# Sums of squares by TensorE, and the order of the first pair of weight blocks, in a two-block transformer kernel

## The chip, the cores and the metric

One core of one Trainium2 chip runs the whole program. The metric is the device time of one execution in microseconds (us): 2955.29 is the median of three runs before the change (2952.16 to 2956.52). The engines are TensorE (PE, with its weight loads as PEld), VectorE (DVE), ScalarE (ACT), GpSimd (POOL) and SyncE (SP), which issues most transfers.

## The reference, cut to what matters

Two transformer blocks of two layers each work on 256 tokens `x` and 256 context tokens `ctx` of width 1024, in float32. The part that the change touches is the very first step, the first half of the first feed-forward layer:

```python
def rms_norm(x, g):
    y = x * rsqrt(mean(x * x, axis=-1) + EPS)
    return y * g
def modulate(h, shift, scale):
    return h * (1 + scale) + shift
mod = silu(c) @ w_ada[l] + b_ada[l]              # nine chunks of 1024: shift, scale, gate, ...
a, b = split(modulate(rms_norm(h, g), mod[0], mod[1]) @ w_in, 2)   # w_in is 1024 x 5632
h = h + 0.5 * mod[2] * ((silu(a) * b) @ w_out)
```

Tokens and context have modulations of their own (`c` and `c_ctx`), and the same weights.

## The kernel before

Activations lie transposed: eight tiles `h` of 128 features by 512 columns, the first 256 columns being the tokens (stream 0) and the last 256 the context (stream 1). Products are made in three passes of a reduced-precision type: weight and operand are each split into a high and a low part, `wh`, `wl` and `xnh`, `xnl`, and PE adds high x high (line 346), high weight x low operand (347) and low weight x high operand (348). ACT writes the high parts (316 for weights, 613 for operands), DVE the low parts (317, 614).

The start of the program is written apart, by the class `Start` and `first_pair` (line 758). `load_stream` (1724) has PE transpose the tokens tile by tile (1735), DVE copy each tile into `h` (1736) and `Sumsq.add` form the squares: ACT squares (98, 101), DVE adds the squares up (103) and squares the last tile (106), into buffers of which there are two. `rstd_bc` then sums over features on PE with a column of ones (568), DVE takes the inverse root with three rounds of Newton's method on two columns (580 to 588), and PE spreads it to rows (562).

The modulation's first two chunks are made in four parts, each for two tiles of `h`: PE multiplies 2 MB of `w_ada` by the padded silu (173, tile `ada`), DVE copies the result (176, `adae`), PE turns it (178, `adat`), and DVE adds the bias (184), makes the gain (186) and for two tiles and two streams scales (139, `nt`); then ACT and DVE split the scaled tiles. I call 178 the turn of a part. The products of the first pair of weight blocks with these two tiles follow: two blocks, two halves of 128 output columns each, in the accumulators `fa`.

A scheduler sets each engine's order of the whole program from a timing model of its own; `issue_after` adds the demand that what is issued inside it stands behind a given instruction of the same engine. Before the change the first weights' split stands behind the end of the roots (`chain_end`), and the parts 1 to 3 behind the spread rows (`rows_done`); how products and modulation interleave is the scheduler's choice. Behind the pair come the second pair's products, `evac` (739) and the background task `ada_tasks`, which makes the other seven chunks on DVE (481, 483). Accumulators of PE come from one pool of five buffers.

Of the kernel before, what the change touches and what calls it, by code (L numbers as in the profile page):

```python
# [9 lines left out]
F32 = mybir.dt.float32  # L10
F32R = mybir.dt.float32r
I32 = mybir.dt.int32
AF = mybir.ActivationFunctionType
ALU = mybir.AluOpType
AX = mybir.AxisListType

P = 128
D = 1024
KT = 8
T = 512  # L20
EPS = 1e-6
D_FF = 2816
# [120 lines left out]
class Start(Norm):  # L143


    def prepare(self):
# [5 lines left out]
        nc.vector.tensor_copy(self.pad[:, :, 0:2], b.silu)  # L152
        self.gs = b.spool.tile([P, KT, 2], F32, tag="gs", name=b.name("gs"), bufs=2)

    def rstd(self, s):
        self.rb[s] = self.b.rstd_bc(self.accs[s], D)

    def load(self, g):
        w = self.b.a["w_ada"][0]
# [5 lines left out]
    def part(self, g, raws):  # L165

        b, nc = self.b, self.b.nc
        ps = b.psum("ada", "ada")
        for j, raw in enumerate(raws):
            for k in range(KT):  # L170
                for i in range(2):
                    q = 32 * (2 * j + i)
                    nc.tensor.matmul(ps[q : q + 32, :P], self.pad[:, k, :], raw[:, k, P * i : P * i + P],
                                     start=(k == 0), stop=(k == KT - 1), tile_position=(0, q))
        ev = b.ntmp("adae")
        nc.vector.tensor_copy(ev[:, :P], ps[:, :P])
        pt = b.psum("adat")
        nc.tensor.transpose(pt[:, :P], ev[:, :P], b.ident)
        mod = b.mod[self.key]
        for j in range(2):  # L180
            o = KT * j + 2 * g
            src = pt[:, 64 * j : 64 * j + 64].rearrange("p (i r) -> p i r", i=2)[:, :, 0:2]
            bias = b.vec("b_ada0", o, 2).unsqueeze(2).broadcast_to([P, 2, 2])
            nc.vector.tensor_tensor(mod[:, o : o + 2, :], src, bias, op=ALU.add)
        gain = b.vec(*self.gain, KT)[:, 2 * g : 2 * g + 2]
        nc.vector.scalar_tensor_tensor(self.gs[:, 2 * g : 2 * g + 2], mod[:, KT + 2 * g : KT + 2 * g + 2, :], 1.0,
                                       gain.unsqueeze(2).broadcast_to([P, 2, 2]), op0=ALU.add, op1=ALU.mult)
        for k in (2 * g, 2 * g + 1):
            for s in self.streams:
                self.tile(s, k, self.rb[s])  # L190
        if 2 * g + 2 == KT:
            b.mod_done.update(((self.key, self.sh_chunk), (self.key, self.sc_chunk)))
# [43 lines left out]
class Builder:  # L236
# [70 lines left out]
        self.nc.sync.dma_start(v, src.rearrange("(k p) n -> p k n", p=P))  # L307
        return raw

    def split_weight(self, raw, kts, n):  # L310
        w = kts * n
        h = self.wspl.tile([P, 2048], F32R, tag="wh", name=self.name("wh"))
        l = self.wspl.tile([P, 2048], F32R, tag="wl", name=self.name("wl"))

        for i0, i1 in self.pieces(w, 1024):
            self.nc.scalar.activation(h[:, i0:i1], raw[:, i0:i1], AF.Copy)  # L316
            self.nc.vector.tensor_tensor(l[:, i0:i1], raw[:, i0:i1], h[:, i0:i1].bitcast(F32), op=ALU.subtract)  # L317
        r = lambda t: t[:, :w].rearrange("p (k n) -> p k n", n=n)
        return Weight(r(h), r(l))

# [283 lines left out]
    def split_from(self, t, dst, k, c0, c1, bias=None):  # L604

        nc = self.nc
        h = dst.H(k, c0, c1)
        l = dst.L(k, c0, c1)
        if bias is None:
            nc.scalar.activation(h, t, AF.Copy)  # L610
            nc.vector.tensor_tensor(l, t, h.bitcast(F32), op=ALU.subtract)
        else:
            nc.scalar.activation(h, t, AF.Identity, bias=bias)  # L613
            nc.vector.scalar_tensor_tensor(l, t, bias, h.bitcast(F32), op0=ALU.add, op1=ALU.subtract)  # L614

    def norm_of(self, key, gname, gi, sh_chunk, sc_chunk, streams):

# [92 lines left out]
    def ffn(self, l, which, streams, x, nxt, side=None, start=None):  # L710
        nc = self.nc
# [5 lines left out]
        w_in = a[f"w_ffn{which}_in"][l]  # L717
# [15 lines left out]
        def weights(t):  # L733
            return [self.weight(w_in[:, o + t * P : o + t * P + 256], KT, 256) for o in (0, D_FF)]
# [23 lines left out]
        def first_pair():  # L758

            raws = [start.load(0)]  # L760
            with self.tc.issue_after(self.chain_end.ins):
                ws = weights(0)
            raws += [start.load(i) for i in range(1, 4)]
            pp = [[self.psum("fa") for _ in ws] for _ in range(2)]
            for i in range(4):
                with self.tc.issue_after(self.rows_done.ins) if i else nullcontext():
                    start.part(i, raws[i])
                for j in range(2):
                    for w, ps in zip(ws, pp[j]):
                        self.mm_feat(ps, w, j * P, x, 0, T, (2 * i, 2 * i + 1), i == 0, i == 3)  # L770
            for j in range(2):
                evac(j, *pp[j], 0, T)

# [4 lines left out]
        for t in (0, 2, 4, 6, 8):  # L778
            if start is not None and t == 0:
                first_pair()  # L780
            else:
                pair(t, t == 0)
                if start is not None and t == 2:
                    self.load_vectors(2, len(self.groups), nc.sync)
# [1087 lines left out]
```

## Time and profile before

| what | value |
|---|---|
| median of 3 runs | 2955.29 us |
| the profiled execution's own time | 2955.05 us |
| its span | 2953.3 us |
| PE busy | 2885.5 us, 98% |
| DVE busy | 2122.6 us, 72% |
| ACT busy | 1086.5 us, 37% |
| mean granted clock of PE | 0.988 |

The page of the profile is one execution; its own time lies 1.75 us above its span. Times of rows count from the span's start. In a timeline each row is a run of like instructions: start, duration, engine, line, operation, output and inputs, and in brackets the idle time of the engine just before it and what ended that. The chain of waits takes 91% of the span on PE. Granted clock 1.00 is 2.4 GHz, 0.50 is 1.2 GHz.

### The profile page before, as it was taken

The numbers are of one execution on the slowest core, as the hardware profiler recorded it, in microseconds if no ns is written. First come the engines' busy times: TensorE is split into PE (matmuls) and PEld (weight loads), VectorE is DVE, ScalarE is ACT, GpSimd is POOL, SyncE is SP. The second block draws the span as 40 slices with busy tenths as digits, with TensorE's granted clock in tenths as the row PEclk, the third lists the DMA queues.
The fourth block names the chain that finished last, engine by engine and source line by source line (L and its number), as shares of the span: only waits on it lengthen the run. The fifth ranks groups of instructions, "written<-read, shape, count | busy, mean of one in ns | idle before, by whom it ended". The sixth has DMA issues, their size and how long they took to land.

```text
span 2953.3 us, 44554 instructions
## 1 busy us (share of the span) xinstructions
PE 2885.5 (98%) x17874; PEld 2480.1 (84%) x17874; DVE 2122.6 (72%) x4323; ACT 1086.5 (37%) x1986; POOL 47.8 (2%) x83
## 2 busy tenths in 40 slices
PE   8999999999999999999989999999999999999998
PEld 6788899688888888888969999886888889996998
DVE  7878768869887698777885675437697785537665
ACT  3223235543222232222653443335342223435443
POOL 0000000000000000000000000011000000011000
PEclk9999999999999999999999999999999999999999
DMA  7655523214654446454323554202255651312553
GB/s 251 206 179 197 174 73 112 62 58 159 219 182 168 135 155 210 166 191 150 104 96 115 180 167 133 76 1 68 86 172 171 199 174 56 117 53 73 171 187 111
DMA packets 357611, 410.27 MB, mean 139 GB/s; under 512 B 24066, under 2 KB 297884, under 8 KB 357404
## 3 DMA queue, kind: packets, MB, share of 16 engines
q1 hardware_dynamic: 353512, 403.63, 41.7%
q10 hardware_dynamic: 3892, 3.78, 0.4%
q8 instruction: 141, 2.31, 0.3%
q14 instruction: 66, 0.54, 0.1%
HBM read 406.34 MB, written 1.05 MB: 138 GB/s over the span
## 4 chain that ended last, share of the span: by engine, by line
PE 91%; DVE 5%; ACT 2%; DMA 1%; issue 1%; SPq 0%; POOL 0%; ACTq 0%; DVEq 0%; POOLq 0%
PE pj L346 14%; PE pj L347 13%; PE pj L348 13%; PE fa L346 9%; PE fa L347 9%; PE fa L348 9%; PE pf L346 2%; PE pf L348 2%; PE pf L347 2%; PE sc L826 2%; PE po L858 1%; DVE wl L317 1%; PE pj L360 1%; PE pj L361 1%; PE pj L362 1%; PE pt L847 1%
## 5 line engine op out<-in xcount | busy, mean ns | idle before, releaser
L316 ACT ACTIVATE wh<-wr 128x1024 fp32r<-128x1024 f32 (+3 forms) x542 | 525.8, 1017 | 860.5 <-PE pj L347 480.1
L317 DVE TENSOR_TENSOR wl<-wr,wh 128x1024 fp32r<-128x1024 f32 (+3 forms) x542 | 624.6, 1175 | 175.0 <-ACT wh L316 172.6
L483 DVE SCALAR_TENSOR_TENSOR ad<-wr,silu,ad 128x512 f32<-128x512 f32 x784 | 547.8, 744 | 16.2 <-DMA wr<-in_w_ada_dram 16.1
L347 PE MATMUL fa<-xnl,wh 128*128 128x512 f32 (+1 forms) x1472 | 522.0, 357 | 1.9 <-DVE xnl L614 1.9
L348 PE MATMUL fa<-xnh,wl 128*128 128x512 f32 (+1 forms) x1472 | 522.1, 357 | 1.1 <-DVE wl L317 1.1
L346 PE MATMUL fa<-xnh,wh 128*128 128x512 f32 (+1 forms) x1472 | 518.7, 359 | 3.8 <-ACT xnh L613 3.0
L346 PE MATMUL pj<-gh,wh 128*128 128x256 f32 (+1 forms) x1372 | 458.0, 335 | 0.0
L347 PE MATMUL pj<-gl,wh 128*128 128x256 f32 (+1 forms) x1372 | 456.6, 333 | 0.0
L348 PE MATMUL pj<-gh,wl 128*128 128x256 f32 (+1 forms) x1372 | 456.4, 333 | 0.0
L346 PEld LDWEIGHTS fa<-xnh,wh 128*128 128x128 f32 x1472 | 274.1, 188 | 49.7 <-ACT xnh L613 4.5
L348 PEld LDWEIGHTS fa<-xnh,wl 128*128 128x128 f32 x1472 | 276.7, 188 | 44.8 <-DVE wl L317 1.5
L347 PEld LDWEIGHTS fa<-xnl,wh 128*128 128x128 f32 x1472 | 276.6, 188 | 44.3 <-DVE xnl L614 2.9
L346 PEld LDWEIGHTS pj<-gh,wh 128*128 128x128 f32 x1372 | 259.5, 189 | 28.5 <-ACT wh L316 1.6
L348 PEld LDWEIGHTS pj<-gh,wl 128*128 128x128 f32 x1372 | 259.3, 189 | 27.2
L347 PEld LDWEIGHTS pj<-gl,wh 128*128 128x128 f32 x1372 | 259.6, 189 | 26.0 <-issue 0.2
L347 PE MATMUL pj<-xnl,wh 128*128 128x256 f32 (+1 forms) x824 | 259.1, 319 | 1.9 <-DVE xnl L614 1.9
L346 PE MATMUL pj<-xnh,wh 128*128 128x256 f32 (+1 forms) x824 | 256.7, 320 | 2.7 <-ACT xnh L613 2.6
L348 PE MATMUL pj<-xnh,wl 128*128 128x256 f32 (+1 forms) x824 | 259.1, 319 | 0.0
L347 PEld LDWEIGHTS pj<-xnl,wh 128*128 128x128 f32 x824 | 155.1, 189 | 13.6 <-DVE xnl L614 2.5
L346 PEld LDWEIGHTS pj<-xnh,wh 128*128 128x128 f32 x824 | 153.4, 190 | 14.8 <-ACT xnh L613 3.3
L348 PEld LDWEIGHTS pj<-xnh,wl 128*128 128x128 f32 x824 | 155.4, 189 | 12.0
L706 DVE SCALAR_TENSOR_TENSOR h<-pj,mod,h 128x256 f32<-128x256 f32 x144 | 66.5, 480 | 112.2 <-PE pj L348 112.1
(374 smaller groups left out, 4252.6 us busy)
## 6 DMA issues: line engine op xcount, KB each, us to landing
wr<-in_w_ada_dram SPq DMA_DIRECT2D x112, 1024.0 KB, 5.1
wr<-in_w_ffn_in_dram SPq DMA_DIRECT2D x88, 1024.0 KB, 5.2
wr<-in_w_mlp_dram SPq DMA_DIRECT2D x64, 1024.0 KB, 5.5
wr<-in_w_ffn_out_dram SPq DMA_DIRECT2D x32, 1024.0 KB, 5.0
wr<-in_w_in_dram SPq DMA_DIRECT2D x20, 1024.0 KB, 5.2
wr<-in_w_ffn_out_dram SPq DMA_DIRECT2D x16, 768.0 KB, 5.5
wr<-in_w_mix_in_dram SPq DMA_DIRECT2D x12, 1024.0 KB, 5.3
ar<-in_w_ada_dram SPq DMA_DIRECT2D x8, 1024.0 KB, 12.4
```

The source lines that it names most:

```text
L316: self.nc.scalar.activation(h[:, i0:i1], raw[:, i0:i1], AF.Copy)
L317: self.nc.vector.tensor_tensor(l[:, i0:i1], raw[:, i0:i1], h[:, i0:i1].bitcast(F32), op=ALU.subtract)
L346: nc.tensor.matmul(o, wh, x.H(k, c0, c1), start=st, stop=False)
L347: nc.tensor.matmul(o, wh, x.L(k, c0, c1), start=False, stop=False)
L348: self.last_mm = nc.tensor.matmul(o, wl, x.H(k, c0, c1), start=False, stop=en)
L360: nc.tensor.matmul(ps_ap, xh, w.h[:, kw, n0:n1], start=st, stop=False)
L361: nc.tensor.matmul(ps_ap, xh, w.l[:, kw, n0:n1], start=False, stop=False)
L362: nc.tensor.matmul(ps_ap, xl, w.h[:, kw, n0:n1], start=False, stop=en)
L483: nc.vector.scalar_tensor_tensor(acc[:, j], raw[:, k - k0], s[:, k, j : j + 1], acc[:, j], op0=ALU.mult, op1=ALU.add)
L706: self.nc.vector.scalar_tensor_tensor(self.h[m][:, e0:e1], ps[:, e0 - c0 : e1 - c0], gate[:, m, s : s + 1], self.h[m][:, e0:e1], op0=ALU.m ...
L826: nc.tensor.matmul(ps[:, :w], q_ap(q0), k_ap(k0 * P, (k0 + nk) * P), start=True, stop=bias is None)
L847: nc.tensor.transpose(pt[:, k * P : (k + 1) * P], p[:, k * P : (k + 1) * P], self.ident)
```

## The change

`Start` gets an `add` of its own: ACT squares every tile, and PE sums each tile's squares at once into the stream's `nm` accumulator, so that DVE neither squares nor adds. In `first_pair` part 0 now stands ahead of the weights' split in the program; the high part of the second block is split behind the last high operand of part 0 on ACT, and the low parts of both behind its last low operand on DVE. The products are written out in a set order: for each part all with high weights, then the next part of the modulation, then half of those with low weights, the turn, and the other half.

```diff
+    def add(self, s, k):
+        b = self.b
+        if k == 0:
+            self.accs[s] = b.psum("nm", "nm")
+        sq = b.sqtmp()
+        b.nc.scalar.activation(sq, b.h[k][:, 256 * s : 256 * s + 256], AF.Square)
+        b.token_sums(self.accs[s], sq, k == 0, k == KT - 1)
+
     def rstd(self, s):
-        self.rb[s] = self.b.rstd_bc(self.accs[s], D)
+        b, ps = self.b, self.accs[s]
+        self.rb[s] = b.rstd_rows(ps, b.rstd_cols(ps, [], D))
...
-        nc.tensor.transpose(pt[:, :P], ev[:, :P], b.ident)
+        self.turned = nc.tensor.transpose(pt[:, :P], ev[:, :P], b.ident)
...
-    def split_weight(self, raw, kts, n):
+    def split_weight(self, raw, kts, n, after=(None, None)):
+        behind = lambda i: self.tc.issue_after(i.ins) if i is not None else nullcontext()
...
         for i0, i1 in self.pieces(w, 1024):
-            self.nc.scalar.activation(h[:, i0:i1], raw[:, i0:i1], AF.Copy)
-            self.nc.vector.tensor_tensor(l[:, i0:i1], raw[:, i0:i1], h[:, i0:i1].bitcast(F32), op=ALU.subtract)
+            with behind(after[0]):
+                self.nc.scalar.activation(h[:, i0:i1], raw[:, i0:i1], AF.Copy)
+            with behind(after[1]):
+                self.nc.vector.tensor_tensor(l[:, i0:i1], raw[:, i0:i1], h[:, i0:i1].bitcast(F32), op=ALU.subtract)
...
         def first_pair():
             raws = [start.load(0)]
-            with self.tc.issue_after(self.chain_end.ins):
-                ws = weights(0)
+            wr = [self.load_raw(w_in[:, o : o + 256], KT, 256) for o in (0, D_FF)]
             raws += [start.load(i) for i in range(1, 4)]
+            start.part(0, raws[0])
+            ws = [self.split_weight(r, KT, 256, (self.split_h if i else None, self.split_l)) for i, r in enumerate(wr)]
             pp = [[self.psum("fa") for _ in ws] for _ in range(2)]
+            def products(i, which, ks=(0, 1)):
+                for k in [2 * i + e for e in ks]:
+                    for w, col in zip(ws, range(2)):
+                        for j in range(2):
+                            wk = (w.l if which == 2 else w.h)[:, k, j * P : j * P + P]
+                            xk = (x.L if which == 1 else x.H)(k, 0, T)
+                            self.last_mm = nc.tensor.matmul(pp[j][col], wk, xk, start=(k == 0 and which == 0), stop=(k == KT - 1 and which == 2))
             for i in range(4):
-                with self.tc.issue_after(self.rows_done.ins) if i else nullcontext():
-                    start.part(i, raws[i])
-                for j in range(2):
-                    for w, ps in zip(ws, pp[j]):
-                        self.mm_feat(ps, w, j * P, x, 0, T, (2 * i, 2 * i + 1), i == 0, i == 3)
+                products(i, 0)
+                products(i, 1)
+                if i < 3:
+                    with self.tc.issue_after(self.last_mm.ins):
+                        start.part(i + 1, raws[i + 1])
+                products(i, 2, (0,))
+                with self.tc.issue_after(start.turned.ins):
+                    products(i, 2, (1,))
```

The order of instructions moves at three places. On ACT, where the first weights and operands are split, before:

```order
L101 ACTIVATE sq_232<-h_95 128x256
L101 ACTIVATE sq_239<-h_96 128x256
L101 ACTIVATE sq_246<-h_97 128x256
L316 ACTIVATE wh_287<-wr_285 128x1024 x2
L316 ACTIVATE wh_295<-wr_293 128x1024 x2
L613 ACTIVATE xnh_359<-nt_357,mod_104 128x256
L613 ACTIVATE xnh_359<-nt_363,mod_104 128x256
L613 ACTIVATE xnh_359<-nt_367,mod_104 128x256
```

and now, with `wh_371` and `wh_377` for the first and second weight block and `sq` for the squares of the second stream:

```order
L161 ACTIVATE sq_252<-h_96 128x256
L329 ACTIVATE wh_371<-wr_297 128x1024 x2
L161 ACTIVATE sq_260<-h_97 128x256
L627 ACTIVATE xnh_355<-nt_353,mod_104 128x256
L161 ACTIVATE sq_268<-h_98 128x256
L627 ACTIVATE xnh_355<-nt_359,mod_104 128x256
L627 ACTIVATE xnh_355<-nt_363,mod_104 128x256
L627 ACTIVATE xnh_355<-nt_367,mod_104 128x256
L329 ACTIVATE wh_377<-wr_299 128x1024 x2
```

The first block's split stands ahead of the last two squares, and the second block's behind the four operands of part 0.

On PE, from the turn of part 1 (`adat_434`), before:

```order
L178 MATMUL adat_434<-ident,adae_432 128x128
L173 MATMUL ada_479<-ar_305,pad_114 32x128 x5
L347 MATMUL fa_313<-xnl_360,wh_287 128x512
L348 MATMUL fa_313<-xnh_359,wl_288 128x512
L347 MATMUL fa_314<-xnl_360,wh_295 128x512
L348 MATMUL fa_314<-xnh_359,wl_296 128x512
L347 MATMUL fa_315<-xnl_360,wh_287 128x512
L348 MATMUL fa_315<-xnh_359,wl_288 128x512
L347 MATMUL fa_316<-xnl_360,wh_295 128x512
L348 MATMUL fa_316<-xnh_359,wl_296 128x512
L173 MATMUL ada_479<-ar_305,pad_114 32x128 x11
L173 MATMUL ada_479<-ar_306,pad_114 32x128 x2
```

and now, from the same turn (`adat_438`), where `wl` are products with low weights and the following ones use the high operands that part 1 gives:

```order
L188 MATMUL adat_438<-ident,adae_436 128x128
L788 MATMUL fa_383<-xnh_355,wl_372 128x512
L788 MATMUL fa_385<-xnh_355,wl_372 128x512
L788 MATMUL fa_384<-xnh_355,wl_378 128x512
L788 MATMUL fa_386<-xnh_355,wl_378 128x512
L788 MATMUL fa_383<-xnh_355,wh_371 128x512
L788 MATMUL fa_385<-xnh_355,wh_371 128x512
L788 MATMUL fa_384<-xnh_355,wh_377 128x512
L788 MATMUL fa_386<-xnh_355,wh_377 128x512
```

Part 2 of the modulation (`ada_479`), which stood among the products, is gone from here; it now stands behind all products of part 1 with high weights.

On DVE, behind the first pair, before (`ad` is the modulation in the background, `th` frees an accumulator `fa`, `wl` is the low part of the next weight):

```order
L483 SCALAR_TENSOR_TENSOR ad_722<-wr_723,silu,ad_722 128x512 x5
L483 SCALAR_TENSOR_TENSOR ad_722<-wr_733,silu,ad_722 128x512 x4
L741 SCALAR_TENSOR_TENSOR th_641<-th_641,fa_313 128x512
L483 SCALAR_TENSOR_TENSOR ad_722<-wr_733,silu,ad_722 128x512 x2
L317 TENSOR_TENSOR wl_666<-wr_663,wh_665 128x1024
L742 TENSOR_TENSOR th_641<-th_641,fa_314 128x512
L483 SCALAR_TENSOR_TENSOR ad_722<-wr_733,silu,ad_722 128x512
L317 TENSOR_TENSOR wl_666<-wr_663,wh_665 128x1024
```

and now, where `fa_383` is the first of the pair's accumulators:

```order
L497 SCALAR_TENSOR_TENSOR ad_734<-wr_735,silu,ad_734 128x512 x5
L497 SCALAR_TENSOR_TENSOR ad_734<-wr_745,silu,ad_734 128x512 x4
L331 TENSOR_TENSOR wl_678<-wr_675,wh_677 128x1024
L497 SCALAR_TENSOR_TENSOR ad_734<-wr_745,silu,ad_734 128x512
L331 TENSOR_TENSOR wl_678<-wr_675,wh_677 128x1024
L755 SCALAR_TENSOR_TENSOR th_653<-th_653,fa_383 128x512
L497 SCALAR_TENSOR_TENSOR ad_734<-wr_745,silu,ad_734 128x512
L755 SCALAR_TENSOR_TENSOR th_661<-th_661,fa_385 128x512
```

The step that reads the first accumulator stood ahead of the next weight's low part, and now stands behind both halves of it.

## Rows read from the trace of the kernel before

**Rows 1.** Timeline, TensorE, 4 to 30 us: start, duration, instruction, idle before.
```profile
...
4.80 5.15 PE L1735 MATMUL xt<-ident,tok 128*128 128x128 f32 x26
10.19 1.10 PE L1735 MATMUL xt<-ident,tok 128*128 128x128 f32 x6 [0.23 <-DVE h L1736]
...
14.38 0.61 PE L568 MATMUL nm<-sumto,acc 128*128 128x1 f32 x4 [0.80 <-DVE acc L103]
14.85 0.58 PE L568 MATMUL nm<-sumto,sq 128*128 128x1 f32 x4
...
20.73 0.69 PE L562 MATMUL nm<-ident,rs 128*128 128x128 f32 x4
24.36 1.22 PE L562 MATMUL nm<-ident,rs 128*128 128x128 f32 x4 [2.94 <-DVE rs L588]
25.52 4.56 PE L173 MATMUL ada<-ar,pad 128*32 128x128 f32 x64
...
```

**Rows 2.** Busy us per stretch (PE, PEld, DVE, ACT, POOL), clock, DMA.
```profile
...
20.00:25.00 5.00, 2.06 (x15) 1.87 (x16) 3.77 (x18) 3.31 (x4) 0.00 (x0) 0.64 1.09 366
...
90.00:95.00 5.00, 5.00 (x17) 3.94 (x16) 2.62 (x9) 2.64 (x3) 0.00 (x0) 0.69 0.92 263
...
```

**Rows 3.** Timeline, VectorE, 20 to 23 us: second root, first scaling.
```profile
...
20.91 0.16 DVE L580 TENSOR_SCALAR ms<-nm 128x2 f32<-128x2 f32 x1 [0.35 <-PE nm L568]
...
21.69 0.16 DVE L588 SCALAR_TENSOR_TENSOR rs<-nt,rs 128x2 f32<-128x2 f32 x1
21.77 0.47 DVE L139 SCALAR_TENSOR_TENSOR nt<-h,gs,nm 128x256 f32<-128x256 f32 x1
...
22.73 0.35 DVE L587 SCALAR_TENSOR_TENSOR nt<-rs,ms 128x1 f32<-128x1 f32 x2
...
```

**Rows 4.** Timeline, ScalarE, 21 to 38 us: the second weight split and operands.
```profile
...
21.32 2.00 ACT L316 ACTIVATE wh<-wr 128x1024 fp32r<-128x1024 f32 x2 [0.41 <-DMA wr<-in_w_ffn_in_dram]
...
35.09 1.31 ACT L613 ACTIVATE xnh<-nt,mod 128x256 fp32r<-128x256 f32 x3 [4.50 <-DVE nt L139]
37.05 0.51 ACT L613 ACTIVATE xnh<-nt,mod 128x256 fp32r<-128x256 f32 x1 [0.66 <-DVE nt L139]
...
```

**Rows 5.** Timeline, TensorE, 30 to 51 us: first products, turns, part 3.
```profile
...
30.00 1.19 PE L346 MATMUL fa<-xnh,wh 128*128 128x512 f32 x4
...
33.80 0.27 PE L178 MATMUL adat<-ident,adae 128*128 128x128 f32 x1
...
46.76 0.33 PE L178 MATMUL adat<-ident,adae 128*128 128x128 f32 x1 [0.39 <-DVE adae L176]
47.02 3.29 PE L173 MATMUL ada<-ar,pad 128*32 128x128 f32 x64
...
```

**Rows 6.** Timeline, TensorE, 67 to 91 us: behind the first pair.
```profile
...
67.02 0.39 PE L346 MATMUL fa<-xnh,wh 128*128 128x512 f32 x1
...
68.75 0.50 PE L348 MATMUL fa<-xnh,wl 128*128 128x512 f32 x1 [1.10 <-DVE wl L317]
...
87.72 0.26 PE L415 MATMUL pv<-ident,rows 48*128 48x48 f32 x1 [1.83 <-DVE th L741]
88.64 0.47 PE L346 MATMUL fa<-xnh,wh 128*128 128x512 f32 x1 [0.66 <-DVE cols L416]
...
90.04 0.63 PE L348 MATMUL fa<-xnh,wl 128*128 128x512 f32 x1
90.47 0.63 PE L346 MATMUL fa<-xnh,wh 128*128 128x512 f32 x1
...
```

**Rows 7.** Chain of waits, 31 us: start, duration, what.
```profile
...
31.19 0.23 PE fa L347
...
```

**Rows 8.** Timeline, VectorE, 54 to 69 us: behind part 3's turn.
```profile
...
54.34 0.23 DVE L184 TENSOR_TENSOR mod<-adat,cols 128x4 f32<-128x4 f32 x2 [2.62 <-PE adat L178]
...
59.41 6.05 DVE L483 SCALAR_TENSOR_TENSOR ad<-wr,silu,ad 128x512 f32<-128x512 f32 x9
...
67.47 1.22 DVE L317 TENSOR_TENSOR wl<-wr,wh 128x1024 fp32r<-128x1024 f32 x1
...
```

More of the change, by code (lines that the diff above doesn't have):

```diff
@@ L612, in split_from @@
         else:
-            nc.scalar.activation(h, t, AF.Identity, bias=bias)
-            nc.vector.scalar_tensor_tensor(l, t, bias, h.bitcast(F32), op0=ALU.add, op1=ALU.subtract)
+            self.split_h = nc.scalar.activation(h, t, AF.Identity, bias=bias)
+            self.split_l = nc.vector.scalar_tensor_tensor(l, t, bias, h.bitcast(F32), op0=ALU.add, op1=ALU.subtract)
     def norm_of(self, key, gname, gi, sh_chunk, sc_chunk, streams):
```

## The prediction

> **What bounds the kernel now.** I read the granted clock and the busy times by stretch first, then the instructions of TensorE (PE) in order of time over the first 95 us, then those of VectorE (DVE) and ScalarE (ACT) in the same stretch, and last the chain of waits. The change touches nothing behind the first pair of weight blocks, so the question is when PE, which is busy nearly without a break from then on, gets through the start. What the reader is to see: PE begins the transposes of the tokens at 4.80 us and is through them at 11.3 [rows 1]. It then waits: for the squares that DVE adds up, and most of all for the second stream's inverse root, so that between 20 and 25 us it is busy 2.06 of 5 us and its granted clock falls to a mean of 0.64, which is partly the lower of its two levels, 1.2 GHz [rows 2]. The second stream's sums have landed at 20.9 us, where DVE begins the root [rows 3]; the rows of that root stand on PE at 24.36, after 2.94 us of idle time [rows 1]. In between DVE waits on ACT, which holds the second weight block's split (2.00 us from 21.32, itself 0.41 us late by a transfer) ahead of the first operand [rows 4]. PE then does part 1 of the modulation in 4.56 us, partly at the low clock [rows 1], where part 3 takes 3.29 at the full one, and the first product of the pair starts at 30.00 [rows 5]. From there to 67.02, where the second column's products begin, PE hardly stops: the idle row is 0.39 us at 46.76 [rows 5, 6].
>
> **The change, part by part.** All terms are late (+) or early (-) of PE against this execution, whose span is 2953.3 us and whose own time is 2955.05, 0.24 under the median of 2955.29.
>
> A, the norm. DVE loses 12 additions and 2 squarings, PE gets 16 pairs of one-column sums instead of 4. A pair costs 14.85 - 14.38 = 0.47 us [rows 1], so the additional work on PE is 12 x 0.47 = 5.6 us. PE's queue up to the last sum is: transposes 5.15 + 1.10, 16 x 0.47 = 7.5, part 0 of the modulation 3.3 (as part 3, rows 5), its turn 0.27, the first stream's rows 0.69 [rows 1, 5], 18.0 in all, from 4.80 to 22.8 if PE never stops. It will stop: ACT's list has both halves of the first weight split (2.00, as for the second in rows 4) ahead of the last two squares, and only two square buffers exist, so ACT cannot run ahead. Between no stop and the whole 2.00 I take 1.2, nearer to the latter, since PE has little else to do in that time: last sum at 24.0, against 20.9. The gain is behind it. The root, now undisturbed, is 0.94 us to the end of its first round (20.91 to 21.85) [rows 3] and two rounds of 0.35 + 0.16 with 0.06 of gaps, 2.1 in all; then the rows 1.22 (low clock, as in rows 1), the scaling 0.47 [rows 3], the operand 0.51 [rows 4] and 0.3 of hand-overs: the first product at 28.6, 1.4 us earlier than 30.00. But part 1 of the modulation, done before the first product so far, now stands behind 16 products: at the full clock 3.29. A is 3.3 - 1.4 = +1.9 us (bounds +0.9 and +3.4, from the two ends of the stop and from 1.2 or 0.7 for the rows).
>
> The Trainium skill's "TensorE: Matmul & The Clock Gate", section "LDWEIGHTS (loading the stationary operand)", speaks against such sums: a weight load costs its 128 columns, some 107 ns, however little is streamed. With two matmuls a pair and two loads for each of them I estimate 12 x 4 x 0.107 = 5.1 us from it, where the row gives 5.6; by that figure A would be some 0.6 less.
>
> B, the clock. PE is nearly idle from 24.0 to 28.6, as it was from 21.4 to 24.4 [rows 1], so the first products will again run at the lower level. There they start 0.43 us apart (90.04 to 90.47) instead of 0.23 [rows 6, 7]. In the earlier case part 1 lost 4.56 - 3.29 = 1.27 us, so 2.5 us of it ran at half rate, and the 1.2 us of rows before it, 3.7 in all; 3.7 us at 0.43 are 8.6 products, which lose 1.7 us. Some of it is hidden, since these products wait for low parts of the operand and for the second weight split, which ACT now does after the operands. B is +1.0, between 0 and +1.8.
>
> The same page, section "HAM oscillation — how this bites in real kernels", says that idle gaps between bursts bring the low clock back. If one-column sums count as activity, the tile-wise sums would keep the clock up to 24, and B would be 0; no row here shows what such sums count for.
>
> C, the set order. In each of the four parts the turn of the modulation is now followed by four products with the low part of the weights, and then by the products that need the operand made from that very turn. From the turn's start at 33.80 the operand of both streams takes until 36.0 (second of three operations from 35.09) for the first tile and 37.56 for the second [rows 4, 5], that is 2.2 and 3.76 us. PE covers 0.27 + 4 x 0.23 = 1.1, waits 1.1, does four products (0.9) and waits 0.6 again. That is 1.7 in parts 1 and 2, 3.4 in all; at part 3 the next pair's products, 18 of them or 4.1 us, stand in between and cover it. So far the next part of the modulation was the cover, cut up among the products. In exchange the 0.39 at 46.76 goes, and two of five breaks between modulation and products, some 0.2 each (four products took 1.19 behind such a break at 30.00, where 3 x 0.23 + 0.39 is 1.08, and this on both sides). C is +2.6, between +1.4 and +3.4.
>
> A to C put PE at 67.02 + 5.5 = 72.5 where the second column's products begin.
>
> D, the buffer behind the pair. The first of those products needs an accumulator that DVE frees. DVE's list from part 3's turn to the twelfth product of the modulation in the background is unchanged: 54.34 to 65.46, 11.1 us [rows 8]. Then it freed the accumulator at once; now two halves of the next weight's low part and one more background product stand ahead: 2 x 1.22 + 0.67, and 0.67 for the freeing step itself [rows 8], 3.8. The turn of part 3 ends 4 + 48 products before the second column, 12 us, at 60.5. So the accumulator is free at 75.4, 2.9 after PE wants it, where PE lost 1.10 to a low part so far [rows 6]. D is +1.8; were the buffer another one, long free, it would be -1.1, and +3.0 is the other end, if the old wait came on top.
>
> E, the next stall. So far PE waited 1.83 us at 87.7 and 0.66 at 88.6 for DVE [rows 6], and then ran at a mean clock of 0.69 over 5 us [rows 2], which is 3.1 us at the half level and 1.5 lost. Its work from 67.02 to that wait is 17.8 without the 1.10, so it would be there at 75.4 + 17.8 = 93.2. DVE by then has 21 operations of 0.67 and four of 1.22 behind the freed buffer, at most 19.0, or 94.4; since such operations overlap a little I take 17.5, 92.9. The old wait of 2.5 falls to some 0.8, mostly for late transfers, and with it the low clock half of the times. E is -2.4, between -4.0 and 0.
>
> Nothing else moves by more than an instruction or two. The additions taken from DVE are worth nothing by themselves, since PE and ACT now set the pace there; the low parts of the first weights, moved behind the operands, are ready before PE asks (four of 1.22 from about 30, the first of them needed at 35).
>
> Sum: 1.9 + 1.0 + 2.6 + 1.8 - 2.4 = +4.9. Behind this stretch PE has no slack to give it back. 2955.05 + 4.9 = 2960.0 us.
>
> **The rivals.**
> 1. The start really gets shorter: the sums hide between the transposes, nothing stops at ACT and the clock stays up. For it: PE now idles 2.94 us in one row [rows 1]. Then A is -0.6 (first product at 26.1, and 3.3 to make up for), B 0, C +1.4, D -1.1, E -3.5: -3.8, or 2951.3 us. Against it: only two square buffers, and a weight split ahead of two squares. Chance 0.20, a third of it beyond 0.2% early.
> 2. VectorE takes over as the bound and the clock falls once more: PE waits 2.9 us at the buffer for the second column, and the low clock follows it as it followed the 2.5 at 88.6, for 1.5 us; the later wait stays as it is. 5.5 + 1.8 + 1.5 + 0.2 = +9.0, or 2964.1 us. It decides if A to C exceed some 4 us, so that part 3's turn is late. Against it: with PE late, DVE has time to catch up elsewhere. Chance 0.25.
> 3. It does nothing: PE's lost time and DVE's cancel, because DVE, which has the same work and hardly a pause from 54.34 to 68.7 [rows 8], sets the end of this stretch in both kernels. 2955.0 us. Against it: this list of DVE's cannot start before part 3's turn, which is late. Chance 0.12.
>
> **How the numbers follow.** The forecast has 0.43: 2960.0 us, its own range 2956 to 2963 with the bounds of A to E against each other. Differences within 0.2%, 5.9 us, cannot be told from no change. Faster by more: 0.06, from rival 1. Slower by more: 0.33, which is most of rival 2 and a quarter of the forecast. Within: 0.61. The range reaches into rivals 1 and 2: 2952 to 2966 us.
>
> **What would show it.** Step A: the last one-column sum ends at about 24 us and the first product starts near 28.6. B: the granted clock is low for some us behind that. C: PE rows with idle time of about 1.1 and 0.6 before the products that follow the turns of parts 1 and 2, released by ACT's operand. D: an idle of 2 to 3 us near 72, released by DVE's first step on the first pair's accumulator. E: the idle near 87 gone or short. A first product before 27, no idle behind the turns, or a second column that begins before 68 would make it wrong.

## The result, and the profile after

The changed kernel takes 2967.05 us (median of 10 runs, 2961.45 to 2977.95) against 2952.81 (10 runs, 2948.29 to 2956.52): ratio 1.0054, 95% interval 1.0041 to 1.0067. It is slower, by 14 us where 5 were forecast, and above the range. Its runs also spread further, with a standard deviation of 6.6 us against 2.5. The profiled execution took 2967.79 us, span 2966.1.

TensorE (PE) over the first 46 us, answering to [rows 1, 5]: start, duration, instruction, idle time before it and what ended it.

```profile
...
5.12 3.25 PE L1764 MATMUL xt<-ident,tok 128*128 128x128 f32 x14
8.16 0.85 PE L582 MATMUL nm<-sumto,sq 128*128 128x1 f32 x4
8.88 0.67 PE L1764 MATMUL xt<-ident,tok 128*128 128x128 f32 x2
...
16.73 3.19 PE L183 MATMUL ada<-ar,pad 128*32 128x128 f32 x26
...
32.31 1.87 PE L582 MATMUL nm<-sumto,sq 128*128 128x1 f32 x8 [0.19 <-ACT sq L161]
36.37 1.23 PE L576 MATMUL nm<-ident,rs 128*128 128x128 f32 x4 [2.20 <-DVE rs L602]
38.71 2.07 PE L788 MATMUL fa<-xnh,wh 128*128 128x512 f32 x4 [1.11 <-ACT xnh L627]
40.58 1.91 PE L788 MATMUL fa<-xnl,wh 128*128 128x512 f32 x4
42.29 1.91 PE L788 MATMUL fa<-xnh,wh 128*128 128x512 f32 x4
44.00 1.47 PE L788 MATMUL fa<-xnl,wh 128*128 128x512 f32 x4
45.40 3.29 PE L183 MATMUL ada<-ar,pad 128*32 128x128 f32 x64
...
```

The reader is to see durations here, not waits. A pair of sums takes 0.72 us from its start to the next (8.16 to 8.88) where a pair in [rows 1] took 0.47; 26 records of the modulation take 3.19 us at 16.73, and 64 of the same kind take 3.29 at 45.40; the first products start 0.43 us apart, later ones 0.23. Up to nearly 45 us everything runs at the lower of PE's two levels, 1.2 GHz. The kernel before left that level during its transposes (26 in 5.15 us, then 6 in 1.10 [rows 1]). The clock column of the busy times by stretch does not say so, as it reads 1.00 there: it has nothing to show ahead of the first change of level that was recorded, so that durations have to be read beside it. The trace's own list of levels agrees with them: in every run here its first entry is the higher level, and it begins at 44.8 us in this execution, at 7.7 us in the profiled execution of the kernel before. I call that the rise.

```profile
...
20.00:25.00 5.00, 5.00 (x40) 4.23 (x42) 0.68 (x4) 0.83 (x2) 0.00 (x0) 1.00 1.09 365
40.00:45.00 5.00, 5.00 (x13) 3.85 (x13) 4.63 (x5) 1.35 (x2) 0.00 (x0) 1.00 0.12 32
45.00:50.00 5.00, 5.00 (x74) 4.17 (x73) 0.33 (x2) 0.00 (x0) 0.00 (x0) 1.00 1.01 347
85.00:90.00 5.00, 3.18 (x14) 2.64 (x15) 5.00 (x8) 2.01 (x2) 0.00 (x0) 1.00 0.52 172
90.00:95.00 5.00, 5.00 (x24) 4.09 (x23) 5.00 (x8) 1.86 (x3) 0.00 (x0) 1.00 0.57 186
...
```

VectorE (DVE) and ScalarE (ACT) between the last sums and the first product, answering to [rows 3, 4]; first ACT, then DVE:

```profile
...
29.96 1.99 ACT L329 ACTIVATE wh<-wr 128x1024 fp32r<-128x1024 f32 x2
31.86 0.40 ACT L161 ACTIVATE sq<-h 128x256 f32<-128x256 f32 x1
...
38.15 1.31 ACT L627 ACTIVATE xnh<-nt,mod 128x256 fp32r<-128x256 f32 x3 [5.19 <-DVE nt L139]
...
```

```profile
...
34.21 0.16 DVE L594 TENSOR_SCALAR ms<-nm 128x2 f32<-128x2 f32 x1 [1.04 <-PE nm L582]
...
36.16 0.16 DVE L602 SCALAR_TENSOR_TENSOR rs<-nt,rs 128x2 f32<-128x2 f32 x1
...
```

The root takes 2.1 us, as forecast; it begins at 34.21 instead of 24. The weight split stands ahead of the last squares, as forecast, but PE is then still working off sums, and waits 0.19 us for it.

PE behind the turns, at the second column and at the old stall, answering to [rows 6]; and DVE's list ahead of the accumulator, answering to [rows 8]:

```profile
...
62.95 1.20 PE L788 MATMUL fa<-xnh,wh 128*128 128x512 f32 x4 [1.04 <-ACT xnh L627]
64.52 1.19 PE L788 MATMUL fa<-xnh,wh 128*128 128x512 f32 x4 [0.37 <-ACT xnh L627]
...
86.82 0.50 PE L360 MATMUL fa<-xnh,wh 128*128 128x512 f32 x1 [2.83 <-DVE th L755]
...
105.34 0.47 PE L360 MATMUL fa<-xnh,wh 128*128 128x512 f32 x1 [0.66 <-DVE cols L430]
...
```

```profile
...
83.15 1.23 DVE L331 TENSOR_TENSOR wl<-wr,wh 128x1024 fp32r<-128x1024 f32 x1
84.29 0.74 DVE L497 SCALAR_TENSOR_TENSOR ad<-wr,silu,ad 128x512 f32<-128x512 f32 x1
84.95 1.22 DVE L331 TENSOR_TENSOR wl<-wr,wh 128x1024 fp32r<-128x1024 f32 x1
86.09 0.68 DVE L755 SCALAR_TENSOR_TENSOR th<-th,fa 128x512 f32<-128x512 f32 x1
...
```

C, D and E of the prediction stand here nearly as forecast: waits of 1.04 and 0.37 behind a turn, 2.83 at the accumulator behind the two halves of the next low part, and 0.66 left of the old stall, with no low clock behind it (1.00 from 85 to 95).

What the start costs as a whole is read further on, at an instruction that both kernels have and that no wait precedes: four transposes of a weight in the first mixer. Before, then after:

```profile
L1130 PE MATMUL wsT<-ident,sg x4: 273/273/273, 535.2 to 535.5; 128*128 128x128 f32 x4
```

```profile
L1159 PE MATMUL wsT<-ident,sg x4: 272/272/273, 550.3 to 550.6; 128*128 128x128 f32 x4
```

PE is 15.1 us late there, and the span ends 12.8 late. "Late at the weight's transposes" below is always the start of these four less 535.2, one execution against one. Up to them the levels on record are the lower one for 10.2 us in the kernel before (6.8 from 21.4 and 3.4 from 89.7) and never in this execution. Behind them both kernels fall to the lower level for some us at a time, at places that differ between executions of one kernel.

**Taking out the recorded clock.** These later stretches make the times of one kernel vary by more than the question is worth. Each run lists its mean recorded clock; the 34 runs of the kernel before beside the first experiments lie on 2928.6 us + 2172 us x (1 - clock) within 1.2 us (standard deviation), those beside the next two sets on 2929.0 + 2107 x and 2929.6 + 2079 x, within 1.9 and 1.6. "Above the line" below is a run's time less the line of its set; the ten runs of the result, beside which no clock of the kernel before is listed, are set against the first line. This height holds what the recorded clock does not, and so a low rate ahead of the first recorded change. A run lists its clock to 0.001, which is some 2 us on these lines.

The 22 runs of the changed kernel (10, and 12 more below) then fall apart: 7 stand 3.3 to 4.9 us above the line, 11 stand 8.8 to 11.9, and 4 stand 16.5 to 19.6. The profiled one is the highest.

### The profile page after: what moved, and what is told of

It reads as the page before. It is cut to its first block, busy times and chain, and to the rows that moved or that the text cites. A ratio compares the mean times of both kernels' runs of the same rounds, so it can differ in the third digit from the quotient of the medians.

```text
span 2966.1 us, 44646 instructions
## 1 busy us (share of the span) xinstructions
PE 2897.5 (98%) x17922; PEld 2492.2 (84%) x17922; DVE 2118.9 (71%) x4309; ACT 1088.2 (37%) x1988; POOL 47.9 (2%) x83
## 4 chain that ended last, share of the span: by engine, by line
PE 92%; DVE 5%; ACT 2%; DMA 1%; issue 1%; SPq 0%; POOL 0%; ACTq 0%; DVEq 0%; POOLq 0%
PE pj L360 14%; PE pj L361 13%; PE pj L362 13%; PE fa L360 9%; PE fa L361 9%; PE fa L362 9%; PE pf L360 2%; PE pf L362 2%; PE pf L361 2%; PE sc L855 2%; PE po L887 1%; DVE wl L331 1%; PE pj L374 1%; PE pj L375 1%; PE pj L376 1%; PE pt L876 1%
## 5 line engine op out<-in xcount | busy, mean ns | idle before, releaser
L360 PE MATMUL fa<-xnh,wh 128*128 128x512 f32 (+1 forms) x1440 | 509.3, 358 | 6.7 <-ACT xnh L627 3.2
L361 PE MATMUL fa<-xnl,wh 128*128 128x512 f32 (+1 forms) x1440 | 509.2, 356 | 1.7 <-DVE xnl L628 1.7
L362 PE MATMUL fa<-xnh,wl 128*128 128x512 f32 (+1 forms) x1440 | 509.6, 356 | 0.0
L360 PEld LDWEIGHTS pj<-gh,wh 128*128 128x128 f32 x1372 | 258.6, 189 | 28.6 <-ACT wh L329 1.6
```

Of the source, the lines that this page charges most:

```text
L360: nc.tensor.matmul(o, wh, x.H(k, c0, c1), start=st, stop=False)
L361: nc.tensor.matmul(o, wh, x.L(k, c0, c1), start=False, stop=False)
L362: self.last_mm = nc.tensor.matmul(o, wl, x.H(k, c0, c1), start=False, stop=en)
```

## The experiments

Theory T1: the loss is the time at which PE comes to its higher rate. T2: the work of the sums and their waits. T3: the order of products and DVE's order.

Each result gives the median, its ratio to the kernel before of the same set with the 95% interval, how far the runs stand above the line, and how late the profiled execution is at the weight's transposes. The code is cut to the lines that matter.

**First set: parts of the change, and two ways to a higher rate.** Kernel before: 2955.69 us (34 runs).

The old norm in the changed kernel (`Start.add` taken out, and this line as before):
```
-        self.rb[s] = b.rstd_rows(ps, b.rstd_cols(ps, [], D))
+        self.rb[s] = self.b.rstd_bc(self.accs[s], D)
```


> The changed kernel with the norm as before (squares added by VectorE, four pairs of sums), but the new order of weights and products. Theory T1: the loss is the TensorE rate at the start, because transposes cut up by one-column sums did not bring the engine to its higher rate before 45 us; with the old norm the rate rises near 8 us as before, the first product starts at 27 to 31 us (38.7 in the changed kernel), the rest is C + D + E of the prediction: 2953 to 2959 us, 8 to 14 under the changed kernel. Theory T2: it is the work of the sums and their waits for two square buffers; the same time here, so this run does not part T1 from T2. Theory T3: the set order of products and the accumulator's wait cost most; then still 2962 or more.

2966.19 us, ratio 1.0037 (1.0023 to 1.005); 4.3 to 7.2 above the line, one group; the weight's transposes at 542.0, 6.8 late. The rise is at 10.7 us, the first product starts at 25.80:

```profile
...
25.80 2.07 PE L778 MATMUL fa<-xnh,wh 128*128 128x512 f32 x4 [1.11 <-ACT xnh L617]
...
38.66 1.21 PE L778 MATMUL fa<-xnh,wh 128*128 128x512 f32 x4 [1.05 <-ACT xnh L617]
...
73.64 0.50 PE L350 MATMUL fa<-xnh,wh 128*128 128x512 f32 x1 [2.83 <-DVE th L745]
93.88 0.26 PE L419 MATMUL pv<-ident,rows 48*128 48x48 f32 x1 [2.68 <-DVE th L745]
95.46 0.47 PE L350 MATMUL fa<-xnh,wh 128*128 128x512 f32 x1 [1.32 <-DVE cols L420]
...
```

The spread goes when the new norm goes, as T1 says; the order stays dear, as T3 says, since with PE early the old stall grows (2.68 and 1.32) instead of shrinking. As a time the expectation of T1 was missed: the medians hold the later stretches of low clock too (in this execution the granted clock is 0.72 from 2060 to 2080 and 0.76 from there to 2100).

The new norm alone in the kernel before:
```
+    def add(self, s, k):   # as in the change
-        self.rb[s] = self.b.rstd_bc(self.accs[s], D)
+        self.rb[s] = b.rstd_rows(ps, b.rstd_cols(ps, [], D))
```


> The kernel before with the sums by TensorE tile by tile alone; weights and products in the old order. T1: one-column sums at 0.85 to 1.0 us a pair as in the changed kernel, second stream's rows near 36 us instead of 24.4, and part 1 of the modulation still ahead of the first product, at the lower rate (6 us instead of 4.56): first product at about 43 us, the time 2963 to 2969. T2: the same start, and the same time. T3: the norm alone costs little: under 2958.

2952.73 us, ratio 0.9986 (0.9977 to 0.9995), but 0.0 to 12.1 above the line, with a median of 3.5: the spread comes with the norm, and the lower time comes of a higher recorded clock (mean 0.991 against 0.988). PE has the same instructions in the same order as in the changed kernel up to the second root, and in the profiled execution it reaches the higher rate behind the first pair of sums, with the rise at 8.8 us:

```profile
...
4.95 3.25 PE L1745 MATMUL xt<-ident,tok 128*128 128x128 f32 x14
7.99 0.85 PE L578 MATMUL nm<-sumto,sq 128*128 128x1 f32 x4
8.71 0.47 PE L1745 MATMUL xt<-ident,tok 128*128 128x128 f32 x2
9.01 0.50 PE L578 MATMUL nm<-sumto,sq 128*128 128x1 f32 x4
...
```

Two transposes take 0.47 us here at 8.71, and 0.67 in the changed kernel at 8.88. The first product starts at 33.49 (43 expected by T1) and the weight's transposes stand at 536.2, 1.0 late. The time is what T3 expected; T1 had taken one execution's rate for a property of the program, and had to be put anew.

Fourteen products of the identity ahead of the tokens, in the changed kernel:
```
+        ps = self.psum("busy", "nm")
+        for _ in range(14):
+            nc.tensor.matmul(ps[:, :P], self.ident, self.ident, start=True, stop=True)
         self.load_vectors(0, 1, nc.sync)
```


> The changed kernel with 14 products of the identity with itself on TensorE before the first transpose, in the 3 us in which it waits for the tokens. T1: the engine comes to its higher rate ahead of or early in the transposes; if it stays there, the pairs of sums take 0.47 us instead of 0.85 to 1.0, the first product starts at 28 to 32 us, and the time is 2954 to 2961. If one-column sums let the rate fall back, the sums are slow again and the time stays above 2962. T2: sums and buffers cost by themselves: first product still behind 35 us, 2964 or more.

2959.39 us, ratio 1.0016 (0.9999 to 1.0033); 3.9 to 8.7 above the line, one group; the rise at 6.3 us, first product at 31.63; 8.0 late at the weight's transposes. The time, the first product and the single group are as T1 has them. But the higher rate did not stay. The first twelve pairs of sums take 0.36 to 0.54 us each; from 23.4 to 37.1 us the level is the lower one again, and the last four pairs take 0.85 to 0.88 each, so the falling back that was named beside T1 came in part:

```profile
...
19.10 1.05 PE L582 MATMUL nm<-sumto,sq 128*128 128x1 f32 x8
...
23.52 3.57 PE L582 MATMUL nm<-sumto,sq 128*128 128x1 f32 x16 [0.63 <-ACT sq L161]
...
```

Whether the sums or the waits of 1.08 and 0.63 us ahead of the fall brought it, this run does not part. The warm-up has its price, since the first transpose starts at 7.33 instead of 5.12.

Sums that stream 128 copies of the ones column:
```
-  matmul(ps[:, 256 + b : 257 + b], sq[...], self.onecol, ...)
+  o = 257 if b else 257 - w          # w = 128
+  matmul(ps[:, o : o + w], sq[...], self.onecol.broadcast_to([P, w]), ...)
```


> The changed kernel with every tile-wise sum streaming 128 copies of the column of ones instead of one (same instruction count, same weight loads, each sum streams 127 columns more). T1: the engine is at its higher rate by 8 to 15 us, as with the transposes alone in the kernel before; though every sum streams more, the first product starts before 33 us and the time falls below 2962. T2: more work per sum, so 2967 to 2972.

2960.75 us, ratio 1.002 (1.0006 to 1.0035); 3.6 to 7.7 above the line, one group; 5.1 late at the weight's transposes. More is streamed in each of the 32 sums, and yet PE is through earlier. The rise is at 9.2 us, and the next fall at 29.7, behind 2.20 and 1.11 us of idle time:

```profile
...
8.56 0.63 PE L1765 MATMUL xt<-ident,tok 128*128 128x128 f32 x2
8.99 0.72 PE L583 MATMUL nm<-sumto,sq 128*128 128x128 f32 x4
...
26.98 0.71 PE L576 MATMUL nm<-ident,rs 128*128 128x128 f32 x4 [2.20 <-DVE rs L603]
28.81 1.97 PE L789 MATMUL fa<-xnh,wh 128*128 128x512 f32 x4 [1.11 <-ACT xnh L628]
...
76.05 0.50 PE L360 MATMUL fa<-xnh,wh 128*128 128x512 f32 x1 [2.83 <-DVE th L756]
...
```

T2 falls. The first product starts at 28.81 (28.6 forecast), the later waits are as forecast, and PE is 5.1 us late in all (4.9 forecast): with an early rise the prediction's sum comes out, though not term by term (B is 2.1 instead of 1.0, C 2.0 instead of 2.6).

**Second set.** Kernel before: 2954.12 us (35 runs). The changed kernel once more:

> The changed kernel itself again, beside the kernels below. In the first twelve runs of it the times, with the recorded clock taken out (the kernel before's 34 runs lie on 2928.6 us + 2172 us x (1 - mean granted clock) within 1.2 us), stand in three groups, 3.4, 9 to 12 and 16.5 to 20 us above that line; the profiled one is the highest, and there TensorE came to its higher rate at 45 us. The kernel with the norm alone has the same instructions on TensorE up to 23 us and came to it at 8.8 us. T1 in its new form: it is left to the execution when the engine comes to its higher rate, and this alone makes the groups: again groups between 3 and 20, and a profile with a rise at a time that answers to its height (near 9 us: 3 to 5 above the line). T3 (the order alone, the same in every run): one group.

2969.2 us, ratio 1.0043 (1.0026 to 1.0059). (The first runs of it were ten, not twelve.) Groups again, 4 runs at 3.5 to 4.9, 7 at 8.9 to 10.9, one at 17.2. The profiled one, 8.9 above, comes to the higher rate behind the 26 records of the modulation, at 19.5 us:

```profile
...
16.43 3.19 PE L183 MATMUL ada<-ar,pad 128*32 128x128 f32 x26
19.56 0.61 PE L582 MATMUL nm<-sumto,sq 128*128 128x1 f32 x4
...
24.01 1.77 PE L582 MATMUL nm<-sumto,sq 128*128 128x1 f32 x12
25.64 0.69 PE L576 MATMUL nm<-ident,rs 128*128 128x128 f32 x4
26.17 0.67 PE L582 MATMUL nm<-sumto,sq 128*128 128x1 f32 x4
27.82 1.87 PE L582 MATMUL nm<-sumto,sq 128*128 128x1 f32 x8 [0.99 <-ACT sq L161]
...
34.22 2.08 PE L788 MATMUL fa<-xnh,wh 128*128 128x512 f32 x4 [1.12 <-ACT xnh L627]
...
```

The first product starts at 34.22, and the weight's transposes stand 10.5 late. Same program, rise at 19.5 or 44.8 us, 8.9 or 19.6 above the line: T1 in its new form. None of the profiles is of the lowest group; that it rises near 9 us is taken from the kernel with the norm alone.

The same execution shows how the rate is lost again. The granted clock falls to 0.50 at 26.4 us, while PE is at work on one-column sums and rows and has had no pause over 0.11 us since its first transpose at 4.83; the wait of 0.99 us comes behind the fall:

```profile
26.40:26.80 0.40, 0.40 (x3) 0.35 (x2) 0.40 (x1) 0.40 (x2) 0.00 (x0) 0.50 1.10 389
```

The norm alone with 8 such products ahead of the tokens (edit as above, `range(8)`):

> The kernel before with the tile-wise sums by TensorE, the old order of weights and products, and 8 products of the identity ahead of the tokens. The norm alone had 2952.7 us and runs 0 to 12 above the line; T1: the warm-up brings the higher rate before 9 us in every run, so all stand within 0 to 3 above the line, and the median is 2947 to 2951, under both kernels. If the spread comes from something else it stays at 0 to 12, 2952 to 2955.

0.9 to 4.0 above the line, one group, the rise at 5.4 us: the spread is gone. The time is 2959.31, ratio 1.0016 (1.0001 to 1.0032), not the 2947 to 2951 hoped for; of the 5.2 us over the kernel before, 2.1 stand above the line and most of the rest is recorded clock (mean 0.9866 against 0.9878). 1.9 late at the weight's transposes, so no gain in the start.

The 14 products and the old order of products, late splits kept (in short):
```
-  products(i, 0); products(i, 1); start.part(i + 1, ...); products(i, 2, ...)
+  start.part(i, raws[i]) behind rows_done; mm_feat(ps, w, j * P, x, 0, T, ...)
```


> The changed kernel with 14 warm-up products (2959.4 us, 6.5 above the line) and the kernel before's order of products and parts of the modulation, the weights' splits left where the change put them (behind the operands). If the set order costs what the waits behind the turns show (1.05 + 0.37 twice) and the accumulator's 2.83, it is 2 to 5 us earlier: 1.5 to 4.5 above the line. If the late splits of the weights are what costs, it stays above 5.5.

2956.3 us, ratio 1.0009 (0.9994 to 1.0025); 2.8 to 8.1 above the line, median 4.6, just past what the order alone should leave; 4.9 late at the weight's transposes against 8.0 with the new order. The order costs up to 3.1 us here: of the two profiled executions the one with the new order also has the longer low stretch (13.7 us from 23.4, against 10.2 from 22.9), and by the medians above the line, which take that out, the difference is 1.9 (6.5 against 4.6).

The 14 products, and DVE's list mended at the accumulator, where `first_freed` is the step that frees the first one:
```
+  ws = [self.split_weight(r, KT, 256, (None, self.first_freed if i else None))
+        for i, r in enumerate(wr)]   # second pair only
```


> The changed kernel with 14 warm-up products and, on VectorE, the second next weight's low part behind the step that frees the first accumulator instead of ahead of it. D of the prediction: the wait of 2.83 us before the second column goes to under 1, but the low part is then later, as in the kernel before (1.10): 1 to 2 us earlier than with the warm-up alone, 4.5 to 5.5 above the line. Rival: VectorE has the same work ahead of the later stall at some 98 us, which takes the gain back: 6 to 7 above the line, as with the warm-up alone.

2956.02 us, ratio 1.0007 (0.9991 to 1.0022); median 5.2 above the line, 5.5 late against 8.0. The wait of 2.83 becomes 0.52, and 0.40 for the low part:

```profile
...
76.40 0.50 PE L360 MATMUL fa<-xnh,wh 128*128 128x512 f32 x1 [0.52 <-DVE th L755]
77.54 0.50 PE L362 MATMUL fa<-xnh,wl 128*128 128x512 f32 x1 [0.40 <-DVE wl L331]
...
```

D is as the prediction has it: of the 2.5 us, 1.9 go at this place, and 0.5 is an earlier start. By the medians above the line it is 1.3.

**Third set.** Kernel before: 2956.52 us (35 runs). The late splits alone in the kernel before (`split_weight` and its call as in the change, the rest as before):

> The kernel before with the late splits of the first two weights alone (behind the operands), the norm and the order of the products as they were. The kernel with the norm alone stood 0 to 2 us above the line with an early rise, the one with old order but late splits and 14 warm-up products 4.6. If the late splits cost 2 us or more by themselves, this stands 2 to 4 above the line; if the rest of the difference is the longer warm-up (TensorE ready 2.2 us later), 0 to 1.5.

2958.32 us, ratio 1.0015 (1.0001 to 1.0028); median 0.7 above the line, 1.1 early at the weight's transposes. The splits show no cost. Between this kernel and the first of the experiments lies the order of products and parts alone: -1.1 against +6.8 at the weight's transposes, 0.7 against 5.8 above the line.

Twelve products of the identity in the wait for the second root, in the kernel before:
```
+  with self.tc.issue_after(self.sum_mm.ins):
+      for _ in range(12):
+          nc.tensor.matmul(ps[:, :P], self.ident, self.ident, start=True, stop=True)
```


> The kernel before with 12 products of the identity on TensorE in the 2.94 us in which it waits for the second stream's root. If the low rate from 21.4 to 28.2 us comes of that idle time, it goes: rows 0.7 instead of 1.22 us, part 1 of the modulation 3.3 instead of 4.56, the first product 1 to 2 us before 30.0, and with the later stall at 87.7 as it is the time 0 to 2 us under the kernel before's. Rival: VectorE, whose list has the turn of part 0 later, gives nothing of it on: within 1 us of the kernel before.

Part 1 of the modulation takes 3.29 us instead of 4.56, the first product starts at 29.61, and the weight's transposes stand 2.6 early. The time does not follow: 2960.28, ratio 1.0013 (1.0000 to 1.0026), 0.9 above the line, and slower by its recorded clock of 0.986.

One background step of DVE moved from the second pair to the fifth, and both edits together:
```
-  self.bg(2)
+  self.bg(1 if start is not None and t == 2 else 3 if start is not None and t == 8 else 2)
```


> The kernel before with one of the two steps of the background modulation at the second pair moved to the fifth pair, so that VectorE has 8 operations of 0.67 us, 5.4 us, less ahead of the end of the first pair. If VectorE's list is what makes PE wait at 68.8, 87.7 and 88.6 us (1.10, 1.83, 0.66, and 1.5 us of low rate behind), these go under 1 us in all and the time is 3 to 5 us under the kernel before's. Rival: the moved step makes VectorE late further on; then the same time as before.

> Both of the two edits before on the kernel before. If their effects add up, 4 to 7 us under the kernel before's time, the fastest of all; if the earlier start only leads into a wait for VectorE, no more than the moved step alone.

2949.67, ratio 0.9991 (0.9976 to 1.0006), and 2955.61, ratio 1.0002 (0.9987 to 1.0016); -1.2 and 0.0 above the line, 1.3 and 1.0 early. The wait at 68.8 goes; near 87 there stay 1.71 and 0.22 us with the moved step alone. That is under half of what the theory wanted, and no version is shown to beat the kernel before: only the norm alone has its interval under 1, and it stands above the line.

## Why the prediction was wrong

**The step that failed is A, and B with it.** A took 0.47 us for a pair of sums and [rows 1]'s times for transposes and part 0, "18.0 in all, from 4.80 to 22.8 if PE never stops". That is the higher rate, and nothing was said of when PE would have it. PE hardly stopped (0.19 us at ACT, where 1.2 was allowed for), and needed until 34.2, because it ran at the lower rate up to 44.8. In the profiled execution A is 8.7 (first product 38.71 against 30.00) + 3.3 for part 1 = +12.0 instead of +1.9. In the second profile it is +7.5, and with wide sums +2.1. The 16 products of part 0 take 45.40 - 38.71 = 6.7 us, 16 x 0.23 would be 3.7: B is +3.0 instead of +1.0; even with an early rise it was 2.1 to 2.7 (5.8 with wide sums, 6.4 with the warm-up), as PE waits 2.20 + 1.11 us right before it. Two slips in the working decide nothing: by the two ends of the stop and of the rows A's bounds are +0.2 and +2.7, not +0.9 and +3.4, and under C PE covers 0.27 + 4 x 0.23 = 1.2 us, not 1.1.

**C and D held.** C is two times 1.04 + 0.37, 2.8 of waits instead of 3.4, and less the prediction's 0.8 of breaks, +2.0 for +2.6. The second column's first product was wanted at 86.82 - 2.83 = 83.99, 17.0 behind 67.02 [rows 6]: 12.0 + 3.0 + 2.0. D: 2.83 - 1.10 = +1.7 for +1.8, shown by mending it.

**E held, and depends on A.** 1.83 us of wait and 1.5 of low clock went, -3.3 for -2.4: PE came later, and DVE had caught up. With the old norm PE was early and the stall grew by 1.5 instead; the order then cost 7.9 us at the weight's transposes, where the warmed-up pair of kernels shows 3.1 (5.1 and 1.9 by the medians above the line). So the order's price is not one number.

Sum: 12.0 + 3.0 + 2.0 + 1.7 - 3.3 = 15.4, where 15.1 was read at 550.3.

**The rivals.** Rival 1 did not occur. It asked that "the clock stays up", and so took for granted, like A, that it is up; when it comes up is what separates the groups. With an early rise the kernel still was not faster. Rival 2's fallen clock behind the accumulator is not in either profile of the changed kernel; it is in the one with wide sums (0.75 from 75 to 80). It was to decide if A to C exceed 4 us; they came to 17.0, and it did not. Rival 3 is out, since DVE's list began later with the late turn.

The prediction weighed the Trainium skill's "TensorE: Matmul & The Clock Gate", section "HAM oscillation — how this bites in real kernels", only for the gap behind the sums. The trace agrees there in part: with the gap filled, the clock from 25 to 30 us is 0.97 instead of 0.68, though 0.69 stays from 20 to 25. In the second profile of the changed kernel the clock fell at 26.4 us without an idle gap ahead of it, so idle time is not all that brings the low level here. The sentence "no row here shows what such sums count for" named the open point, but its price was put into B, on the few us behind the sums, and not on the 18.0 us of A's queue itself.

**What stays open.** Of the 14 to 15 us between the medians, 9 to 10 are above the line. The rest is lower recorded clock (0.986 against 0.988), part of it in the start (13.7 us at the lower level from 26.4 in the second profile, 10.2 us in the first 100 of the kernel before), the rest later, where the instructions are the same. Several experiments show the same without an edit there, one the opposite. Whether the change has a part in that, or 12 runs are too few, was not settled. Open too is what in an execution decides when the rise comes: the runs show that it varies once the new norm is in, and that a warm-up or wider sums bring it early, but not why.

## What to carry to other kernels

When a change puts small matmuls between others at a program's start, first ask at which of TensorE's rates that stretch will run, and price it at both; a duration from a row holds only for the rate of that row. That PE is busy does not say which rate it has. One profile shows one execution: where the runs of a kernel spread more than those of the kernel before, look for what differs between executions before explaining the median. Time lost ahead of a stretch that waits for VectorE is partly given back there, and time won is partly lost there.

## What the runs showed that was not expected

The same instructions on TensorE, with no pause over 0.2 us from 5 us on, left the lower level at 8.8 (the norm alone), 19.5 or 44.8 us by execution, and in one of them fell back to it at 26.4 while still busy with one-column sums. The granted clock read 1.00 throughout the low stretch at the start, and the mean clock that a run lists leaves it out too: the profiled run of the changed kernel has the highest mean of its ten, 0.991, and stands highest above the line. At equal recorded clock the kernel before repeats within 1.2 to 1.9 us (standard deviation), less than half of its spread in time (4.5 to 5.0).
